# Two decoder blocks on one core: operands moved within 256 bytes, the even stage reordered, retention values in three passes

## The chip, the cores and the metric

One Trainium2 chip, one core of it. The metric is the device time of one execution in microseconds; lower is better. Float32 values are split into two parts of a shorter format (float32r), hi and lo, and most products are computed as hi·hi + hi·lo + lo·hi: three TensorE matmuls for each block of 128 rows.

## The reference, cut to what matters

A sequence of 256 tokens of width 1024 goes through a first block of 2 layers and a second of 2 layers; the second carries 256 context tokens beside the 256 latent ones (two streams).

```python
# first block, each of 2 layers
xn = rmsnorm(x, norm_mix[l])
qa..va, qb..vb, qc..vc, qi, ki, wi, gates = split(xn @ w_in[l])
y = g0 * (chunk_band(qa, ka, va) @ w_up_a) + g1 * (diff(qb, kb, vb) @ w_up_b) + g2 * (sparse(qc, kc, vc) @ w_up_c)
x = x + y @ w_out
x = x + memory_cross_attention(rmsnorm(x), mem)
x = x + (silu(h @ w_gate) * (h @ w_up)) @ w_down          # h = rmsnorm(x)

# second block, each of 2 layers; modulate(x) = rms_norm(x, gain) * (1 + scale) + shift
x = x + 0.5 * m2 * swiglu(modulate(x), ffn_a)              # both streams
# layer 0, "even": neighbourhood attention and a hyena operator
a = neighbourhood_attention(q, k, v, k_ctx, v_ctx, rpb)    # latent; the context attends to itself
z = x1 * x2                                                # short convolutions of three projections
b = (long_conv(z, filter) + z * hy_bias) * x0
x = x + m5 * (concat(a, b) @ even_out)
# layer 1: retention, latent stream alone in the output
inner = (q @ k.T) * decay;  o = inner @ v                  # both directions and the context's keys
x = x + m5 * ((silu(g) * groupnorm(o)) @ ret_out)
x = x + 0.5 * m8 * swiglu(modulate(x), ffn_b)
```

## The kernel before

**Layout.** Activations lie feature-major: 128 partitions of features, tokens along the free axis. A projection to feature-major output keeps the weights still and streams the activations (mm3, L296: lines 300, 301, 302, `fm_pair`, `fm2`, `fm2_split`, `down`), 256 columns where one stream runs and 512 where both do. A projection to token-major output (`tm_proj`, L405: lines 418 to 420) keeps the activations still and streams 512 columns of the weights; v of every attention, q, k and v of the even stage and v of retention go this way.

**Weights.** One list, `plan` (L1047), fixes the order of all 674 weight tiles of 128 x 1024. `Weights.pump` (L180) issues a tile's load on SP's queue (`raw`, 4 buffers), casts it to `whi` on ACT (L195) and subtracts to `wlo` on DVE (L196), 4 buffers each, as tiles before it are done with.

**Order.** The program is written as generators. `drive` (L265) takes a step of the main line (some 24 matmuls), then a step of a side line (attention, the index, hyena, norms) and of the modulation vectors (`mods`). TensorE runs the instructions in that order. Four PSUM banks (`acc`) hold projections, four (`aux`) all the rest.

**Places of the streamed operands.** They follow from the sizes of the tiles in the order of allocation. Bytes past a multiple of 256 at which the operand starts: `hh`, `hl` of the first block 192; `oh`, `yh`, `xoh` (attention outputs and mixed values) 64 in layer 0 and 96 in layer 1; `hidh`, `hidl` (gated hidden values) 64 in layer 0, 192 in layer 1 and 192 in the second block; `hh2`, `hl2` (named hh, hl in the profile, since they take that name) of the second block 224; `whi`, `wlo` 128, still or streamed. Consecutive 128-row blocks of an operand are 1024 or 2048 bytes apart, so the place is the same for all of them.

**The even stage** (`even`, L1603). z projections, transposed and handed to `hyena` (L1568) as a side line: a forward transform of 256 points by matmuls, a product with the filter's spectrum F on DVE (L1582 to L1587), an inverse transform (L1595), and z * hy_bias added (L1599). Beside it q, k, v; each of q and k is normed (L1658 to L1673) after its projection. Then neighbourhood attention of four pairs of heads and the context's own of four (`attention`, L536), its first steps beside the four x0 chunks, the rest by itself (L1710); then even_out.

**Retention** (`ret`, L1758). k, q, gates, then v, head by head; `ret_head` (L1857) computes the decays, the scores, the values as float32 matmuls (L1883, two records each), a norm over the head's width, and the gate. Then ret_out (L1846), `add_gated`, squares (`sq2`), and `norm2` (L1300): a sum over partitions on TensorE (L1305), a power on POOL (L341), a broadcast on TensorE (L1314), and `modulate` (L1326) with shift and scale. The last feed-forward stage (`ffn2`, L1394) calls `need_stream(0)` before its first matmul.

Of the kernel before, what the change touches and what calls it, by code (L numbers as in the profile page):

```python
# [17 lines left out]
P = 128  # L18
# [32 lines left out]
def layout(inp):  # L51
# [49 lines left out]
    o["w_mod"] = np.ascontiguousarray(f["w_mod_2"].transpose(0, 2, 1)).reshape(-1, P, D)  # L101
    o["cc"] = np.stack([f["c_2"][0], f["c_ctx_2"]])
# [4 lines left out]
def tables():  # L107
# [43 lines left out]
    o["rpos"] = np.ascontiguousarray(np.stack([np.maximum(i - j, 0), np.maximum(j - i, 0), 1.0 + (i == j), 256 + i - j, 256 - i + j], axis=1)).astype(np.float32)  # L151
# [4 lines left out]
EVEN_ORDER = [c for i in range(4) for c in (12 + 4 + i, 12 + 8 + i)] + list(range(12)) + [12, 13, 14, 15]  # L156
# [13 lines left out]

class Weights:
    S = 4
    R = 4

# [5 lines left out]
    def pump(self, limit=1 << 30):  # L180
        nc = self.nc
        moved = True
        while moved:
# [7 lines left out]
            if self.n_split < min(self.n_dma, self.n_done + self.S):  # L191
                raw = self.raw.pop(self.n_split)
                hi = self.pool.tile([P, 1024], F32R, tag="whi", name="whi", bufs=self.S)
                lo = self.pool.tile([P, 1024], F32R, tag="wlo", name="wlo", bufs=self.S)
# [18 lines left out]
class Prog:  # L213
# [214 lines left out]
    def scores(self, pr):  # L428
# [5 lines left out]
        e = self.att.tile([P, 2, w], F32, tag=pr.tag, name="e", bufs=2)  # L434
# [59 lines left out]
    def values(self, pr):  # L494
# [7 lines left out]
        if pr.rev:  # L502
            self.split(pr.oh.rearrange("p (t n) -> p t n", n=P), pr.ol.rearrange("p (t n) -> p t n", n=P), self.rev(ps[:, :T]))
        else:
            self.split(pr.oh, pr.ol, ps[:, :T])

# [462 lines left out]
    def ffn1(self, l):  # L969
        nc = self.nc  # L970
        x = (self.hh, self.hl)
        with ExitStack() as st:
# [8 lines left out]
            def gate(j, pa, pb):  # L981
                ga = tp.tile([P, 2, T], F32, tag="ga", name="ga")
                sg = tp.tile([P, 2, T], F32, tag="sg", name="sg")
                u = tp.tile([P, 2, T], F32, tag="u", name="u")
# [62 lines left out]
    def plan(self):  # L1047
# [52 lines left out]
        for i in range(16):  # L1100
# [4 lines left out]
    def setup(self):  # L1105
# [8 lines left out]
        nc.gpsimd.memset(self.mhalf, -0.5)  # L1114
        self.modT = [cp.tile([P, 9, 2, KC], F32, name=f"modT{l}") for l in range(2)]
    def setup1(self, st):
# [13 lines left out]
        self.bgain = cp.tile([P, 2], F32, name="bgain")  # L1130

# [104 lines left out]
    def setup2(self):  # L1236
# [5 lines left out]
        self.hl2 = cp.tile([P, KC, 2 * T], F32R, name="hl2")  # L1242

# [56 lines left out]
    def norm2(self, l, n, s, spread=False):  # L1300
# [12 lines left out]
        for t in range(2):  # L1313
            nc.tensor.matmul(ps[:, t * P:(t + 1) * P], rs[:, t:t + 1].to_broadcast([P, P]), self.ident, start=True, stop=True)  # L1314
        yield from self.modulate(l, n, s, lambda h, m: nc.vector.tensor_tensor(h, self.x2[:, m, s * T:(s + 1) * T], ps[:, :T], ALU.mult), spread)
# [9 lines left out]

    def modulate(self, l, n, s, normed, spread=False):  # L1326

        nc = self.nc
        shift, scale = self.need_mod(l, 3 * n), self.need_mod(l, 3 * n + 1)
        g = PAR["norm_gain"] + (l * 3 + n) * KC  # L1330
        gs = self.small2.tile([P, KC], F32, tag="gs", name="gs", bufs=2)
# [598 lines left out]
```

## Time and profile before

| | us |
|---|---|
| median of 3 runs | 2888.71 |
| lowest, highest | 2887.57, 2890.21 |
| the profiled execution | 2887.65 |
| its span, first to last instruction | 2885.7 |
| TensorE busy (18,228 matmuls) | 2855.2 |
| DVE, ACT busy | 2001.3, 1270.0 |

The granted TensorE clock is 0.997 of full speed over the span. Busy times of TensorE overlap, since matmuls are pipelined: an instruction lasts longer than the time until the next can start. How often one starts is read from a stretch in which a single loop runs: its length over the instructions in it.

### The profile page before, as it was taken

The numbers are of one execution on the slowest core, as the hardware profiler recorded it, in microseconds if no ns is written. First come the engines' busy times: TensorE is split into PE (matmuls) and PEld (weight loads), VectorE is DVE, ScalarE is ACT, GpSimd is POOL, SyncE is SP. The second block draws the span as 40 slices with busy tenths as digits, with TensorE's granted clock in tenths as the row PEclk, the third lists the DMA queues.
The fourth block names the chain that finished last, engine by engine and source line by source line (L and its number), as shares of the span: only waits on it lengthen the run. The fifth ranks groups of instructions, "written<-read, shape, count | busy, mean of one in ns | idle before, by whom it ended". The sixth has DMA issues, their size and how long they took to land.

```text
span 2885.7 us, 46572 instructions
## 1 busy us (share of the span) xinstructions
PE 2855.2 (99%) x18228; PEld 2523.8 (87%) x18228; DVE 2001.3 (69%) x3896; ACT 1270.0 (44%) x2002; POOL 77.9 (3%) x137
## 2 busy tenths in 40 slices
PE   8999999999999999999999999999999999999999
PEld 7899999989989988888876988888888888978999
DVE  7767898866878778784657566555887846535655
ACT  7666644677654532222436432123322235423543
POOL 0000000000000000000011000000000000000000
PEclk9999999999999999999999999999999999999999
DMA  7555577655656646553322244442565634522564
GB/s 229 161 163 168 196 237 244 188 146 159 197 174 211 220 152 187 187 185 98 111 73 66 81 146 141 144 153 88 158 188 185 188 92 136 161 68 91 159 187 147
DMA packets 150748, 452.04 MB, mean 157 GB/s; under 512 B 17183, under 2 KB 24936, under 8 KB 149760
## 3 DMA queue, kind: packets, MB, share of 16 engines
q1 hardware_dynamic: 147040, 435.94, 48.7%
q0 software_dynamic: 3344, 12.96, 1.4%
q8 instruction: 143, 2.34, 0.3%
q14 instruction: 77, 0.63, 0.1%
q10 hardware_dynamic: 144, 0.16, 0.0%
HBM read 447.94 MB, written 1.06 MB: 156 GB/s over the span
## 4 chain that ended last, share of the span: by engine, by line
PE 85%; issue 3%; DVE 2%; ACT 1%; POOL 0%; DMA 0%; POOLq 0%; DVEq 0%; ACTq 0%
PE acc L301 25%; PE acc L300 25%; PE acc L302 25%; PE acc L418 2%; PE acc L419 2%; PE acc L420 2%; PE aux L1883 1%; PE aux L489 1%; PE aux L501 1%; PE aux L1578 0%; PE aux L1876 0%; PE aux L442 0%; DVE wlo L196 0%; PE aux L1595 0%; DMA lg<-logit 0%
## 5 line engine op out<-in xcount | busy, mean ns | idle before, releaser
L195 ACT CAST whi<-raw 128x1024 fp32r<-128x1024 f32 x674 | 704.8, 1049 | 1344.4 <-PE acc L301 635.5
L300 PE MATMUL acc<-hh,whi 128*128 128x256 f32 (+1 forms) x3728 | 1167.7, 315 | 5.0 <-ACT hh L308 3.7
L196 DVE TENSOR_TENSOR wlo<-raw,whi 128x1024 fp32r<-128x1024 f32 x674 | 822.5, 1223 | 503.5 <-ACT whi L195 497.3
L301 PE MATMUL acc<-hl,whi 128*128 128x256 f32 (+1 forms) x3728 | 1166.5, 314 | 0.1
L302 PE MATMUL acc<-hh,wlo 128*128 128x256 f32 (+1 forms) x3728 | 1164.5, 314 | 0.0
L300 PEld LDWEIGHTS acc<-hh,whi 128*128 128x128 f32 x3728 | 699.1, 188 | 66.1 <-issue 7.7
L301 PEld LDWEIGHTS acc<-hl,whi 128*128 128x128 f32 x3728 | 701.7, 188 | 50.3 <-issue 0.8
L302 PEld LDWEIGHTS acc<-hh,wlo 128*128 128x128 f32 x3728 | 699.9, 188 | 46.6 <-issue 0.4
L1224 DVE CUSTOM_DVE_ANT_0 mjunk<-mraw,cb 128x512 f32<-128x512 f32 x576 | 396.4, 688 | 32.3 <-DMA mraw<-w_mod 20.9
L302 PE MATMUL acc<-hidh,wlo 128*128 128x256 f32 (+1 forms) x1152 | 370.4, 322 | 0.0
L301 PE MATMUL acc<-hidl,whi 128*128 128x256 f32 (+1 forms) x1152 | 370.3, 321 | 0.0
L300 PE MATMUL acc<-hidh,whi 128*128 128x256 f32 (+1 forms) x1152 | 368.8, 320 | 0.0
L301 PEld LDWEIGHTS acc<-hidl,whi 128*128 128x128 f32 x1152 | 216.3, 188 | 18.5
L300 PEld LDWEIGHTS acc<-hidh,whi 128*128 128x128 f32 x1152 | 216.3, 188 | 18.5
L302 PEld LDWEIGHTS acc<-hidh,wlo 128*128 128x128 f32 x1152 | 216.1, 188 | 16.6
L418 PE MATMUL acc<-whi,hh 128*128 128x512 f32 x320 | 131.7, 411 | 0.0
L420 PE MATMUL acc<-wlo,hh 128*128 128x512 f32 x320 | 127.0, 397 | 0.0
L419 PE MATMUL acc<-whi,hl 128*128 128x512 f32 x320 | 126.6, 396 | 0.0
L1412 DVE TENSOR_TENSOR u<-acc,u 128x512 f32<-128x512 f32 (+1 forms) x88 | 54.8, 624 | 79.6 <-PE acc L302 79.3
L1392 DVE SCALAR_TENSOR_TENSOR x<-acc,modT,x 128x256 f32<-128x256 f32 x136 | 59.6, 478 | 54.7 <-PE acc L302 54.7
L418 PEld LDWEIGHTS acc<-whi,hh 128*128 128x128 f32 x320 | 60.2, 188 | 17.0 <-issue 3.8
L419 PEld LDWEIGHTS acc<-whi,hl 128*128 128x128 f32 x320 | 60.3, 188 | 14.8 <-issue 1.4
(373 smaller groups left out, 2614.7 us busy)
## 6 DMA issues: line engine op xcount, KB each, us to landing
mraw<-w_mod SPq DMA_DIRECT2D x288, 256.0 KB, 3.1
raw<-w_in SPq DMA_DIRECT2D x126, 512.0 KB, 3.6
raw<-w_gu SPq DMA_DIRECT2D x88, 512.0 KB, 4.2
raw<-ffn_a_in SPq DMA_DIRECT2D x88, 512.0 KB, 3.5
raw<-ffn_b_in SPq DMA_DIRECT2D x88, 512.0 KB, 3.5
raw<-ret_in SPq DMA_DIRECT2D x48, 512.0 KB, 3.5
raw<-w_down SPq DMA_DIRECT2D x44, 512.0 KB, 4.1
raw<-ffn_a_out SPq DMA_DIRECT2D x44, 512.0 KB, 3.5
```

Source lines behind the costliest of these rows:

```text
L195: nc.scalar.copy(hi, raw)
L196: nc.vector.tensor_sub(lo, raw, hi.bitcast(F32))
L300: nc.tensor.matmul(out, wh, xh, start=first, stop=False)
L301: nc.tensor.matmul(out, wh, xl, start=False, stop=False)
L302: nc.tensor.matmul(out, wl, xh, start=False, stop=last)
L418: nc.tensor.matmul(o, xh[:, k, ts], wh[:, kk], start=first, stop=False)
L419: nc.tensor.matmul(o, xl[:, k, ts], wh[:, kk], start=False, stop=False)
L420: nc.tensor.matmul(o, xh[:, k, ts], wl[:, kk], start=False, stop=last)
L489: nc.tensor.transpose(pv[:, h, (t - t0) * P:(t - t0 + 1) * P], pr.e[t][:, h, kb * P:(kb + 1) * P], self.ident)
L1224: self.tc.keep_in_program_order(nc.vector.tensor_tensor_reduce(junk, w, cb[:, s, k * 512:(k + 1) * 512], 1.0, 0.0, ALU.mult, ALU.add, accu ...
L1392: nc.vector.scalar_tensor_tensor(xm, ps[:, ts], gate[:, s, m:m + 1], xm, ALU.mult, ALU.add)
L1412: nc.vector.tensor_tensor(u, pb, u, ALU.mult)
```

## The change

- **Places.** Pads (a tile that nothing uses) and a 64-column widening of the split weight tiles put every streamed float32r operand 64 bytes past a multiple of 256. Still operands of weights stay at 128 (`MOVING` adds 48 columns, 192 bytes, to weight tiles that are streamed). `hh` as a still operand goes to 64 with its streaming place.
- **Even stage.** Order q, k, v, then the z projections, then x0. The q projection takes the latent stream first, then the context's. Attention runs beside v and z and writes its output, unsplit, over q; hyena runs beside the x0 chunks, four steps behind each, in halves of 256 features. z * hy_bias goes into the real part of F. even_out begins with the attention's half of its rows.
- **Last feed-forward stage.** Its first two gated units (four weight chunks) are computed from x2 times the gain, not normed, as soon as ret_out is done, with shift as a 257th column (and a zero as a 258th); the row scale of the norm is applied to the PSUM result.
- **Retention.** The scores and v are split, and values are three float32r matmuls. A head's gate comes a step after its values. `ret_out` starts with chunks of heads 0 and 1. `rpos` has two tables in place of five. The first two heads of k are taken out of PSUM stream by stream.
- `ffn1`'s `u` has one buffer in place of two.

```diff
 class Weights:
+    ROOM, MOVING = 64, 48
+    def moves(self, key):
+        n, i = key[0], key[-1]
+        return (n == "w_kv" and i > 1 or n == "w_in" and key[2] in ("va", "vb", "vc")
+                or n == "even_in" and i < 12 or n == "ret_in" and 16 <= i < 32)
...
+                o = self.MOVING if self.moves(self.seq[self.n_split][0]) else 0
+                hi, lo = (self.pool.tile([P, 1024 + self.ROOM], F32R, tag=n, name=n, bufs=self.S)[:, o:o + 1024] for n in ("whi", "wlo"))
...
+def pad(pool, n):
+    pool.tile([P, n // 4], F32, name="pad")
...
+        pad(self.small, 128)       # setup
+        pad(cp, 128)               # setup1
+        pad(cp, 160)               # setup2
+        pad(fp, 224)               # filter_mlp
+        pad(np_, 224)              # even
+            pad(rp, 160)           # ret
...
 # ffn2, the last stage
+                    for j in range(2):
+                        pa, pb = self.head[2 * j:2 * j + 2]
...
+                        nc.vector.tensor_tensor(u, pa[:, :T], self.rsl, ALU.mult)
+                        nc.scalar.activation(sg, u, AF.Sigmoid, bias=sh[:, 0:1])
+                        nc.vector.scalar_tensor_tensor(u, u, sh[:, 0:1], sg, ALU.add, ALU.mult)
+                        t = tp.tile([P, ns], F32, tag="sg", name="ut2")
+                        nc.vector.tensor_tensor(t, pb[:, :T], self.rsl, ALU.mult)
+                        nc.vector.scalar_tensor_tensor(u, t, sh[:, 1:2], u, ALU.add, ALU.mult)
+                        self.split(hh[:, j], hl[:, j], u)
...
 # hyena, each half f of the features of each stream s
+                for kt in range(2):
...
+                    nc.vector.tensor_tensor(t1, pv, F[:, kt, f], ALU.mult)
+                    nc.vector.tensor_tensor(t2, pv, F[:, kt, f, ::-1], ALU.mult)
+                    nc.vector.tensor_tensor(Y[:, 0, kt], t1[:, 0], t1[:, 1], ALU.subtract)
+                    nc.vector.tensor_tensor(Y[:, 1, kt], t2[:, 0], t2[:, 1], ALU.add)
+                    yield
...
+                nc.scalar.copy(zT[:, 2 * s:2 * s + 2, fs], ps.rearrange("p (j t) -> p j t", j=2))
+                yield
...
 # even, the x0 chunks
             for i in range(4):
                 p, = yield from self.fm2([key(i)], x, 2 * T)
+                self.conv(p, i, u[:, i])
+                self.split(oh[:, i], ol[:, i], qT[:, i])
+                for _ in range(4):
+                    next(hy, None)
+                yield
...
 # ret
+            for m in range(2):
+                half(m, 0)
+                yield
+            next(heads)
+            ysplit(3)
...
+                with self.tc.high_priority(200):
+                    self.split_gain(xg[:, 0, m, :T], xg[:, 1, m, :T], self.x2[:, m, :T], gs[:, m:m + 1])
...
+            ws = [self.w.get(("ffn_b", 1, c), KC) for c in (0, NF, 1, NF + 1)]
+            self.head = [self.acc() for _ in ws]
+            for k in range(KC):
+                for (wh, wl), p in zip(ws, self.head):
+                    self.mm3(p[:, :T + 2], (wh[:, k], wl[:, k]), (xg[:, 0, k], xg[:, 1, k]), k == 0, k == KC - 1)
+                yield
...
 # ret_values
-                nc.tensor.matmul(ps, p[:, kt, t * P:(t + 1) * P], v[:, kt], start=kt == 0, stop=kt == 3)
+                nc.tensor.matmul(ps, ph[:, kt, ts], vh[:, kt], start=kt == 0, stop=False)
+                nc.tensor.matmul(ps, ph[:, kt, ts], vl[:, kt], start=False, stop=False)
+                nc.tensor.matmul(ps, pl[:, kt, ts], vh[:, kt], start=False, stop=kt == 3)
```

## Rows read from the trace of the kernel before

**Rows 1.** The page's first part: busy us (share of the span) x instructions of each engine.

```profile
PE 2855.2 (99%) x18228; PEld 2523.8 (87%) x18228; DVE 2001.3 (69%) x3896; ACT 1270.0 (44%) x2002; POOL 77.9 (3%) x137
```

**Rows 2.** The page's fourth part: the chain that ended last, shares by line.

```profile
PE acc L301 25%; PE acc L300 25%; PE acc L302 25%; PE acc L418 2%; PE acc L419 2%; PE acc L420 2%; PE aux L1883 1%; PE aux L489 1%; PE aux L501 1%; PE aux L1578 0%; PE aux L1876 0%; PE aux L442 0%; DVE wlo L196 0%; PE aux L1595 0%; DMA lg<-logit 0%
```

**Rows 3.** Groups by line and form: count | busy us, mean ns | idle before.

```profile
L300 PE MATMUL acc<-hh,whi 128*128 128x256 f32 x2672 | 752.2, 284 | 4.9 <-ACT hh L308 3.7 <-ACT xv L661 1.3
L302 PE MATMUL acc<-hh,wlo 128*128 128x512 f32 x1056 | 418.3, 396 | 0.0
L300 PE MATMUL acc<-hidh,whi 128*128 128x256 f32 x720 | 200.8, 279 | 0.0
L300 PE MATMUL acc<-hidh,whi 128*128 128x512 f32 x432 | 168.0, 389 | 0.0
L418 PE MATMUL acc<-whi,hh 128*128 128x512 f32 x320 | 131.7, 411 | 0.0
```

**Rows 4.** Stretches (us): length, then PE, PEld, DVE, ACT, POOL busy (count), PEclk, DMA.

```profile
455.00:510.00 55.00, 55.00 (x487) 55.00 (x487) 44.80 (x79) 24.39 (x27) 0.00 (x0) 1.00 0.76 239
945.00:1000.00 55.00, 55.00 (x470) 55.00 (x469) 39.80 (x67) 29.82 (x44) 1.21 (x2) 1.00 0.67 217
345.00:450.00 105.00, 105.00 (x894) 105.00 (x893) 98.04 (x167) 50.28 (x57) 0.00 (x0) 1.00 0.74 235
164.00:184.00 20.00, 20.00 (x179) 20.00 (x178) 10.78 (x12) 10.61 (x13) 0.00 (x0) 1.00 0.58 170
186.00:196.00 10.00, 10.00 (x87) 10.00 (x86) 6.96 (x8) 4.14 (x5) 0.00 (x0) 1.00 0.68 203
673.00:682.00 9.00, 9.00 (x78) 9.00 (x78) 5.91 (x7) 3.98 (x5) 0.00 (x0) 1.00 0.58 185
2700.00:2770.00 70.00, 70.00 (x585) 70.00 (x584) 44.90 (x64) 35.84 (x53) 0.00 (x0) 1.00 0.60 184
```

**Rows 5.** The same view of stretches with 512-column matmuls.

```profile
1035.00:1160.00 125.00, 125.00 (x537) 100.55 (x537) 108.08 (x237) 35.22 (x46) 0.00 (x0) 1.00 0.61 184
1170.00:1240.00 70.00, 70.00 (x308) 57.43 (x307) 51.24 (x122) 13.65 (x13) 0.00 (x0) 1.00 0.59 188
2504.00:2532.00 28.00, 28.00 (x121) 22.53 (x120) 6.73 (x7) 7.50 (x9) 0.00 (x0) 1.00 0.32 95
```

**Rows 6.** The same view of the retention values' stretch; the chain of waits there.

```profile
2498.00:2606.00 108.00, 108.00 (x463) 83.37 (x463) 38.76 (x49) 31.29 (x40) 3.19 (x8) 1.00 0.27 80
...
2617.56 6.88 PE aux L1883 x16
```

**Rows 7.** TensorE's timeline where retention ends: start us, us, what.

```profile
2684.35 0.28 PE L302 MATMUL acc<-hh,wlo 128*128 128x256 f32 x1
2687.29 0.61 PE L1305 MATMUL aux<-ones,ssq 128*128 128x1 f32 x4 [2.66 <-DVE ssq L1298]
...
2692.08 1.22 PE L300 MATMUL acc<-hh,whi 128*128 128x256 f32 x4 [1.93 <-ACT hh L308]
```

**Rows 8.** TensorE's waits at the end and at the start of retention.

```profile
PE aux L1897 <- DVE ry L1890: 1.4, 2, 0.7
...
PE acc L300 <- ACT hh L308: 1.7, 2, 1.4
```

**Rows 9.** Stretches again: the end of retention.

```profile
2684.00:2698.00 14.00, 8.38 (x52) 7.79 (x51) 8.01 (x21) 8.09 (x18) 0.70 (x1) 0.76 0.28 81
```

**Rows 10.** DVE's timeline in the hyena steps; groups by line and form.

```profile
1435.80 0.68 DVE L1582 TENSOR_TENSOR hyY<-aux,hyF 128x512 f32<-128x512 f32 x1
...
L309 DVE TENSOR_TENSOR hl<-modh,hh 128x256 fp32r<-128x256 f32 x88 | 34.4, 419 | 8.5 <-ACT hh L308 7.8
L1337 ACT ACTIVATE modh<-modh,modT,gs 128x256 f32<-128x256 f32 x88 | 49.3, 595 | 31.2 <-DVE modh L1315 23.0 <-DVE modh L1284 8.1
```

**Rows 11.** DMA issues at the start of retention: KB each, us to landing.

```profile
lg<-logit POOLq DMA_DIRECT2D x1, 4.0 KB, 9.5
```

**Rows 12.** Stretches again: the attention of the even stage.

```profile
1549.00:1593.00 44.00, 41.57 (x270) 27.50 (x270) 35.56 (x96) 33.45 (x87) 6.70 (x11) 1.00 0.18 54
```

More of the change, by code (lines that the diff above doesn't have):

```diff
@@ L1099, in plan @@
             add(("ret_in", i), a["ret_in"][i])
-        for i in range(16):
+        for i in [0, 2, 1, 3] + list(range(4, 16)):
             add(("ret_out", i), a["ret_out"][i])
@@ L1589, in hyena @@
-            for i in range(0, 4, 2):
+                    for part in range(2):
+                        for t in range(2):
+                            nc.tensor.matmul(ps[:, part * T:(part + 1) * T], self.dft[:, part, t, kt * P:(kt + 1) * P], zT[:, 2 * s + t, fs], start=t == 0, stop=t == 1)
+                    pv = ps.rearrange("p (a c) -> p a c", a=2)
+                    t1, t2 = (self.cp.tile([P, 2, T], F32, tag="conv", name=n, bufs=2) for n in ("ctm", "ctp"))
+                    nc.vector.tensor_tensor(t1, pv, F[:, kt, f], ALU.mult)
@@ L1660, in even, with flip @@
                     gain = self.pcol("na_k_gain", 0) if part else qgain
-                    for t in range(4):
+                    def flip(t, raw, rs, gain, part):
                         r = raw[:, t].rearrange("p (h d) -> p h d", h=8)
@@ L1668, in even @@
                         ts = slice(t * P, (t + 1) * P)
-                        if part == 0:
-                            dst = qT[:, :, ts]
-                            nc.scalar.activation(dst[:, :, ::-1] if t < 2 else dst, pv, AF.Copy, scale=gain)
-                        else:
-                            nc.scalar.activation(k[:, :, ts], pv, AF.Copy, scale=gain)
-                        yield
-                def evac(t, p):
-                    nc.scalar.copy(v[:, t], p)
-                yield from self.tm_proj([("even_in", 8 + i) for i in range(4)], x, 4, evac)
-                while "hyena" not in self.flags:
-                    self.step_side()
-            self.Fst.close()
-            self.att = pool("naatt", st)
+                        dst = k[:, :, ts] if part else qT[:, :, ts]
+                        nc.scalar.activation(dst[:, :, ::-1] if part == 0 and t < 2 else dst, pv, AF.Copy, scale=gain)
+                    for t in range(4):
+                        self.defer(lambda t=t, c=(raw, rs, gain, part): flip(t, *c), 1)
+                yield
+                self.flush_later()
             pairs = []
@@ L1719, in f @@
                         then(s, m0 + i)
-                return f
-            for m0 in (0, 4):
-                yield from self.fm2_split([("even_out", m0 + i) for i in range(4)], x, (0, 1), after(m0))
     def na_bias(self, pr):
@@ new lines, in ret, with evac @@
+            heads = self.ret_heads(rp, rpos, lg, qT, kT, vs, sg)
+            self.side.append(heads)
+            for h in range(4):
+                vs.append(())
+                def evac(t, p):
+                    if t == 0:
+                        vs[h] = tuple(rp.tile([P, 4, 512], F32R, tag=n, name=n, bufs=1) for n in ("rvh", "rvl"))
+                    self.split(vs[h][0][:, t], vs[h][1][:, t], p)
+                yield from self.tm_proj([("ret_in", 16 + 4 * h + i) for i in range(4)], x, 4, evac)
@@ new lines, in ret, with half @@
+            gs = self.mod_gain(1, 2, 0)
+            nc.vector.memset(xg[:, :, :, T + 1:].bitcast(F32), 0.0)
+            self.split(xg[:, 0, :, T], xg[:, 1, :, T], self.need_mod(1, 6)[:, 0])
+            psums = {}
+            def half(m, kg):
+                if kg == 0:
+                    psums[m] = self.acc()[:, :T]
+                wh, wl = self.w.get(("ret_out", 2 * m + kg), KC)
+                for k in range(KC):
+                    self.mm3(psums[m], (wh[:, k], wl[:, k]), (yh[:, 8 * kg + k], yl[:, 8 * kg + k]), kg == k == 0, kg == 1 and k == KC - 1)
+                self.w.done()
@@ L1858, in ret_head, with ret_decays @@
+    def ret_decays(self, h, rp, rpos, lg):
         nc = self.nc
@@ L1907 @@
     pt_bufs = 2
+    e_bufs = 2
+    out = None
     rev = False
```

348 lines of the change are left out of this document (219 added, 129 removed).

## Prediction

> **What bounds the kernel now.** I read the page's busy lines first, then the chain of waits, then TensorE's groups by line, then the stretches of single loops, and last the timeline of the few gaps. TensorE has work under way for 99% of the span [rows 1], and three quarters of the chain that ends last are the three matmuls of one helper, L300 to L302 [rows 2]: the time is nearly the sum of the start-to-start times of 18,228 TensorE instructions. So what decides is how often a matmul can start. I take this from a stretch in which one loop runs: its length over the number of instructions in it, less 2 for those that cross its edges (an instruction lasts some 281 ns and starts every 118, so two are in flight at an edge).
>
> For 256 columns the same down projection takes 55 us / 485 = 113.4 ns in layer 0, where its streamed operand starts 64 bytes past a multiple of 256, and 55 / 468 = 117.5 ns in layer 1, where it starts at 192 [rows 4]. The weights, the loop and the clock (1.00) are alike. The gate loop of layer 0, from 192, takes 105 / 892 = 117.7; layer 1's oh, from 96, 9 / 76 = 118.4; block 2's hh, from 224, 70 / 583 = 120.1. Two rows speak against a plain rule of the address: hh from 192 runs at 20 / 177 = 113.0 in one stretch, and ohc, from 64, at 10 / 85 = 117.6 [rows 4]. There seem to be a fast and a slow steady pattern; from 64 the fast one is the more frequent, from 192 the rare one, and from 96 and 224 there is a third, slower one. For 512 columns [rows 5] the pairs are 125 / 535 = 233.6 from 224, 70 / 306 = 228.8 from 192 and 28 / 119 = 235.3 for streamed weights from 128.
>
> **The change part by part: streamed operands at 64.** Counts are the rows of L300 to L302 times three [rows 3]. Of the 2672 with hh and 256 columns, 1120 lie in block 2 (from 224: gate and up chunks of the split and the last feed-forward stage 544, retention 384, even projections 192), so 1552 lie in block 1 (from 192). Of hidh's 720, 176 in layer 0 start at 64 already. From 192 there are then 1552 + 176 + 368 = 2096 triples, 6288 matmuls; from 224 3360; from 96 176 triples (oh, yh, xoh of layer 1), 528. With 512 columns: 3168 of hh, 1296 of hidh, 960 streamed weights.
> What share from 64 will be fast? In the rows one stretch of two, and 485 of 570 matmuls; I take 0.7, so 0.7 x 113.4 + 0.3 x 117.5 = 114.6 ns. From 192 the rows have 177 of 1537 fast, a mean of 117.1.
> - From 192: 2.5 x 6288 = 15.7 us; none if slow, 23.3 if all are fast.
> - From 224: 5.5 x 3360 = 18.5 us; 8.7 if slow (117.5), 22.5 if fast.
> - From 96: 3.8 x 528 = 2.0 us; 0.5 and 2.6.
> - 512 columns from 64 no row shows. The floor would be twice the fast 256, 226.8; the nearest row is 228.8. I take 228: 5.6 x 3168 = 17.7, 0.8 x 1296 = 1.0, 7.3 x 960 = 7.0, together 25.7 us. The ends are 33 (all at 226.8) and, if the place does nothing for 512, 0. For streamed weights the stationary operand (hh) moves to 64 too, a pair that stands in no row, so a loss isn't excluded there; by the spread of the 512 rows, 6.5 ns, it would be 6 us.
> Sum 61.9 us, between 3 (slow pair, 512 unchanged, the loss of 6) and 81. No work hides this: TensorE is the chain.
> The trace's rows tell the five starts apart. The Trainium skill ("SBUF — State Buffer", Specifications (TRN2)) names a 16-byte line as the unit that costs when it is crossed. All of the starts are multiples of 32 bytes, so by that rule they are alike, this sum is nothing, and what is left is the third rival below; layer 0 against layer 1 [rows 4] speaks against it.
>
> **Retention values in three passes.** Now 64 records of L1883, 16 in 6.88 us [rows 6], 27.5 us. After: 4 heads x 2 x 4 x 3 = 96 matmuls of 512 columns at 228, 21.9 us: 5.6 us less. Added beside it are 24 casts on ACT and 24 subtractions on DVE of 512 (16 for v, where a plain copy was, 8 for p), at 0.69 [rows 10] 16.6 us of DVE, in a stretch of 108 us in which DVE is busy 38.8 and ACT 31.3 [rows 6]: hidden. If it weren't, at most the 16.6 would come back. The start of the heads' steps moves by one step each; the transposes of y now come one step behind the values, so that the two waits for ry, 1.4 us [rows 8], go; for the last head two half chunks of ret_out (48 matmuls, 5.5 us) stand between.
>
> **Last gated unit un-normed.** Now the last matmul of ret_out starts at 2684.35, the first of the last feed-forward stage at 2692.08 [rows 7]: 7.6 us, of which 8 small matmuls take 0.9. The granted clock of that stretch is 0.76 [rows 9]; the next 13 matmuls run at half clock, 13 x 0.1 = 1.3 us more. Together 8.0 us lost. After: four chunks' matmuls (96, of 258 columns) read the scaled, un-normed x and need no norm. In order on TensorE behind the first 12 of them comes the sum of squares, which was ready 2.94 us after the last matmul [rows 7], so it still waits 2.94 - 12 x 0.12 = 1.5 us. The broadcast comes some 36 matmuls in; behind it ACT and DVE have 8 modulated chunks (each an activation of 0.6 and a cast on ACT, two of 0.42 on DVE [rows 10]), some 8 us, then the first gate unit. But the head holds all four acc banks until its gate units read them, and only 60 matmuls (7 us) are left to cover: the next chunk waits some 3 us. So 4.5 of the 8.0 stay: 3.5 us less. If the banks come late by the whole 8 us, 0; if nothing waits, 8.
>
> **Smaller pieces.** Start of retention: TensorE waits 1.7 us for hh [rows 8] behind ACT, which stands at the exponential of lg; lg lands 9.5 us after its issue [rows 11], in one queue behind axC and axS of 256 KB and rpos of 5 x 512 x 4 x 128 bytes, 1280 KB. rpos becomes 512 KB; at that queue's pace (1792 KB in some 9.5 us) lg comes some 4 us earlier and most of the wait goes: 1.5 us less (0 to 1.7). The two products of 8 columns that are added there stand behind the same DMA, off TensorE's path.
> Even stage: the same matmuls of the hyena steps, in other widths. Attention moves beside the value and z projections, where DVE has room. That closes part of the 2.4 us in which TensorE has nothing in 1549 to 1593 [rows 12], and some waits inside it that the busy time covers: 3 us less (0 to 6). In exchange hyena's twelve steps, now one between matmuls of a projection, are issued four at a time after each x0 chunk. An inverse step right behind its forward step waits for two products of 512 and two sums of 256 on DVE: 2 x 0.69 + 2 x 0.42 = 2.2 us [rows 10]. Three such waits bare: 6.6 us, with partial cover 4 more (0 to 9). The direct term's 256 KB and its two sums come in the filter's stage of block 1, beside the cross attention, where F is not yet wanted; the pads are space alone.
>
> **Sum.** 61.9 + 5.6 + 1.4 + 3.5 + 1.5 + 3 - 4 = 72.9 us, against the profiled execution's 2887.65 (span 2885.7 and 1.95 around it): 2814.8. The median of the runs shown, 2888.71, is 1.1 above it: 2816.
>
> **Rivals.**
> 1. The slow pattern stays: from 64 the matmuls settle at 117.5 as ohc does [rows 4], and only the starts at 224 and 96 gain. 8.7 + 0.5 for 256; 512 at the row of 192, 228.8: 4.8 x 3168 + 6.5 x 960 = 21.4. With the 11 us of the other parts 41.6 less: 2847. For it: a loop that begins slow stays slow for its 96 matmuls. Against: layer 0's down projection came out of a slow gate loop and ran fast.
> 2. All settle fast: 81 + 11 less, 2797. For it: 485 matmuls on end. Against: ohc.
> 3. The place of the operand is worth nothing, and the two rates come from something else that differs between the layers: 11 less, 2878.
> 4. Slower: hyena's steps lie bare. All eight forward steps' 2.2 us of DVE and four copies of 0.6 on ACT stand between matmuls: 20 us on the path of the even stage, and the 3 us there are not won. The parts outside that stage give 12.0 (5.6 + 1.4 + 3.5 + 1.5), so it makes the kernel slower from where the operands give less than 8 us; with rival 3 it is 2888.7 - 12 + 20 = 2897. For it: nothing stands between the four steps but what another chunk of x0 lends. Against: each chunk gives 5.5 us of cover, and DVE was busy for 0.81 of the stretch with the most attention in it [rows 12].
>
> **How the numbers follow.** Forecast 0.62 (2816, own range 2797 to 2838), rival 1 0.17, rival 2 and below 0.07, rival 3 0.08, rival 4 0.06. The range for 8 in 10 leaves out the far end of rival 2 and rivals 3 and 4: 2788 to 2866. A measurement of this kernel tells 0.2%, 6 us, from no change. Rival 3 at 11 us is faster by that bound, with a few hundredths of it within: faster 0.91, same 0.03, slower 0.06.
>
> **What would show it.** The stretches of the gate loops: windows of hh with 256 columns at 113 to 115 ns a matmul (right), or at 117.5 throughout (rival 1) or 120 in block 2 (rival 3). 512 columns at 227 to 229 in the feed-forward stages of block 2. L1883's successor at 228 a matmul, with no wait for the split of v. Between ret_out and the last stage two gaps of 1.5 and 3 us in place of 7.6, and a clock of 1.00. In the x0 chunks of the even stage waits of TensorE for hyY: up to four of 2 us is the forecast, eight or more is rival 4. The prediction is wrong where the 512-column matmuls don't move at all, since a third of the sum rests on them without a row.

## The result, and the profile after

The changed kernel takes 2857.46 us (median of 4 runs, 2852.39 to 2860.48), the kernel before in the same job 2889.46: a ratio of 0.9888, with a 95% interval of 0.9871 to 0.9905, 32 us less. The forecast was 73 us less. The time lies inside the range and outside the likeliest case's own one.

The profiled execution takes 2852.39 us. First its page: busy time by engine, answering to [rows 1], and the chain that ended last by line, answering to [rows 2].

```profile
PE 2820.6 (99%) x18196; PEld 2502.3 (88%) x18196; DVE 2018.8 (71%) x3935; ACT 1284.2 (45%) x2030; POOL 76.0 (3%) x131
...
PE acc L313 25%; PE acc L314 25%; PE acc L315 25%; PE acc L431 2%; PE acc L433 2%; PE acc L432 2%; PE aux L514 1%; DVE wlo L209 1%; PE aux L502 1%; ACT whi L208 1%; PE aux L1644 0%; PE aux L2049 0%; PE aux L1631 0%; PE aux L455 0%; ACT modh
```

L313 to L315 are now the three matmuls of the helper, L431 to L433 those with streamed weights. TensorE is still under way for 99%, so the time went, or stayed, in the interval between two starts. The stretches of single loops, columns as in [rows 4]: first 256 columns (layer 0's gates and down projection, layer 1's, block 2's last gates, and the retention gates), then 512 columns as in [rows 5] (hh, hidh, streamed weights), and last the end of retention, as in [rows 9].

```profile
345.00:450.00 105.00, 105.00 (x894) 105.00 (x893) 97.25 (x166) 50.47 (x57) 0.00 (x0) 1.00 0.77 236
455.00:510.00 55.00, 55.00 (x470) 55.00 (x469) 42.79 (x77) 24.38 (x27) 0.00 (x0) 1.00 0.74 230
825.00:930.00 105.00, 105.00 (x928) 105.00 (x927) 88.61 (x129) 51.97 (x58) 0.00 (x0) 1.00 0.71 219
945.00:995.00 50.00, 50.00 (x430) 50.00 (x429) 35.56 (x61) 27.74 (x42) 1.26 (x2) 1.00 0.66 208
2685.00:2740.00 55.00, 55.00 (x487) 55.00 (x487) 37.47 (x55) 27.64 (x42) 0.00 (x0) 1.00 0.64 196
2428.00:2485.00 57.00, 57.00 (x505) 57.00 (x504) 40.93 (x48) 32.59 (x39) 0.00 (x0) 1.00 0.64 194
1030.00:1150.00 120.00, 120.00 (x516) 96.67 (x515) 104.93 (x230) 33.74 (x44) 0.00 (x0) 1.00 0.60 184
1165.00:1230.00 65.00, 65.00 (x281) 52.35 (x280) 48.05 (x113) 11.61 (x11) 0.00 (x0) 1.00 0.58 183
2491.00:2518.00 27.00, 27.00 (x121) 22.48 (x121) 12.32 (x16) 10.71 (x14) 0.00 (x0) 1.00 0.30 93
2673.00:2683.00 10.00, 8.03 (x53) 7.60 (x52) 8.97 (x18) 8.96 (x14) 0.00 (x0) 0.83 0.47 166
```

Every stretch has its streamed operand at 64 now. Three of the loops run at 113 ns (layer 1's gates 105 / 926 = 113.4, block 2's last gates 55 / 485 = 113.4, the retention gates 57 / 503 = 113.3) and two at 117.5 (layer 0's gates 105 / 892 = 117.7, its down projection 55 / 468 = 117.5). Layer 1's down projection, 50 / 428 = 116.8, has both: 117.8 up to 961 us, where four small matmuls break in, then 113.5 up to the next such break at 970 us, then 117.8 again. So 64 does not choose. Layer 0's down projection, fast before [rows 4], is slow now, though its operands have not moved. And 512 columns: 120 / 514 = 233.5, where 233.6 stood [rows 5]; hidh 65 / 279 = 233.0, which was 228.8; only the streamed weights gained, 27 / 119 = 226.9 against 235.3.

All means below are of intervals between successive starts in the trace, without those over 150 ns (256 columns) or 260 (512), in which something was waited for; where the matmuls run by themselves, of the settled later part of a stretch.

Next the waits of TensorE, in three stretches: the end of retention, its start, and the even stage (what is waited for: us in total, times, longest), with the DMA issue of lg, as in [rows 8] and [rows 11].

```profile
PE acc L313 <- DVE u L1454: 1.5, 1, 1.5
PE acc L313 <- ACT whi L208: 0.4, 1, 0.4
...
PE acc L313 <- ACT modh L1365: 2.1, 1, 2.1
PE aux L1335 <- POOL nrs L354: 0.5, 1, 0.5
PE aux L1326 <- DVE ssq L1319: 0.4, 1, 0.4
...
PE aux L455 <- DVE m L472: 1.1, 1, 1.1
PE aux L1335 <- POOL nrs L354: 0.5, 1, 0.5
PE aux L1719 <- DVE naraw L1716: 0.4, 1, 0.4
...
lg<-logit POOLq DMA_DIRECT2D x1, 4.0 KB, 4.1
```

At the end of retention the waits of 2.7, 1.0 and 1.9 us for sums, broadcast and first modulated chunk are gone, and one of 1.5 for the gate unit's product (u) has come. At its start lg lands after 4.1 us, not 9.5, and the wait for hh behind it is gone; the first matmul now waits 2.1 us for the modulated chunk itself (modh), and the sums (ssq) are waited for 0.4 us. In the even stage no wait is for hyY.

### The profile page after: what moved, and what is told of

It is laid out like the page before. It is cut to its first block, busy times and chain, and to the rows that moved or that the text cites. A ratio compares the mean times of both kernels' runs of the same rounds, so it can differ in the third digit from the quotient of the medians.

```text
span 2850.2 us, 46574 instructions
## 1 busy us (share of the span) xinstructions
PE 2820.6 (99%) x18196; PEld 2502.3 (88%) x18196; DVE 2018.8 (71%) x3935; ACT 1284.2 (45%) x2030; POOL 76.0 (3%) x131
## 4 chain that ended last, share of the span: by engine, by line
PE 86%; DVE 2%; ACT 2%; issue 1%; POOL 1%; DMA 0%; ACTq 0%; DVEq 0%; POOLq 0%
PE acc L313 25%; PE acc L314 25%; PE acc L315 25%; PE acc L431 2%; PE acc L433 2%; PE acc L432 2%; PE aux L514 1%; DVE wlo L209 1%; PE aux L502 1%; ACT whi L208 1%; PE aux L1644 0%; PE aux L2049 0%; PE aux L1631 0%; PE aux L455 0%; ACT modh L1365 0%
## 5 line engine op out<-in xcount | busy, mean ns | idle before, releaser
L313 PE MATMUL acc<-hh,whi 128*128 128x256 f32 (+1 forms) x3600 | 1135.1, 316 | 5.6 <-ACT modh L1365 2.1
L314 PE MATMUL acc<-hl,whi 128*128 128x256 f32 (+1 forms) x3600 | 1129.8, 314 | 0.0
L315 PE MATMUL acc<-hh,wlo 128*128 128x256 f32 (+1 forms) x3600 | 1129.0, 314 | 0.0
L313 PEld LDWEIGHTS acc<-hh,whi 128*128 128x128 f32 x3600 | 677.6, 189 | 67.3 <-issue 9.3
L315 PEld LDWEIGHTS acc<-hh,wlo 128*128 128x128 f32 x3600 | 678.4, 189 | 51.7 <-issue 2.7
L314 PEld LDWEIGHTS acc<-hl,whi 128*128 128x128 f32 x3600 | 678.5, 189 | 50.1 <-issue 0.4
L313 PE MATMUL acc<-hidh,whi 128*128 128x256 f32 (+1 forms) x1152 | 371.9, 323 | 0.0
L315 PE MATMUL acc<-hidh,wlo 128*128 128x256 f32 (+1 forms) x1152 | 371.6, 323 | 0.0
L315 PEld LDWEIGHTS acc<-hidh,wlo 128*128 128x128 f32 x1152 | 217.2, 189 | 19.6
L313 PEld LDWEIGHTS acc<-hidh,whi 128*128 128x128 f32 x1152 | 216.7, 188 | 19.8 <-DVE u L1007 0.2
L431 PE MATMUL acc<-whi,hh 128*128 128x512 f32 x288 | 116.1, 403 | 0.0
L433 PE MATMUL acc<-wlo,hh 128*128 128x512 f32 x288 | 113.2, 393 | 0.0
L322 DVE TENSOR_TENSOR hidl<-u,hidh 128x512 fp32r<-128x512 f32 (+1 forms) x110 | 69.4, 632 | 0.8 <-ACT hidh L321 0.7
L321 ACT CAST hidh<-u 128x512 fp32r<-128x512 f32 (+1 forms) x110 | 63.2, 576 | 9.9 <-DVE u L1440 4.9
```

What stands on the lines that cost most here:

```text
L313: nc.tensor.matmul(out, wh, xh, start=first, stop=False)
L314: nc.tensor.matmul(out, wh, xl, start=False, stop=False)
L315: nc.tensor.matmul(out, wl, xh, start=False, stop=last)
L321: self.nc.scalar.copy(hi, src)
L322: self.nc.vector.tensor_sub(lo, src, hi.bitcast(F32))
L431: nc.tensor.matmul(o, xh[:, k, ts], wh[:, kk], start=first, stop=False)
```

## The experiments

The question is where 41 us of the forecast stayed. Theory A, from the comparison: 512-column matmuls gain nothing from the streamed operand's place alone. Theory B: the places gave what was forecast, and another edit took it back.

**Places alone, the rest alone, and the changed kernel again.** The first is the kernel before with:

```diff
+    ROOM, MOVING = 64, 48
-                hi = self.pool.tile([P, 1024], F32R, tag="whi", name="whi", bufs=self.S)
+                o = self.MOVING if self.moves(self.seq[self.n_split][0]) else 0
+                hi, lo = (self.pool.tile([P, 1024 + self.ROOM], F32R, ...)[:, o:o + 1024] for n in ("whi", "wlo"))
-                u = tp.tile([P, 2, T], F32, tag="u", name="u")
+                u = tp.tile([P, 2, T], F32, tag="u", name="u", bufs=1)
+        pad(self.small, 128)
+        pad(cp, 128)
+        pad(cp, 160)
+        pad(fp, 224)
```

Its one buffer for `u` stays in the second kernel too, and no run shows what that alone is worth.

> The kernel before with the streamed operands moved to 64 and nothing else. Theory A (512 columns gain nothing, the 256-column matmuls gain about 31 us, the other edits about 5): 26 to 34 us under the kernel before, near 2858. Theory B (the places gave what was forecast, some 55 to 62 us, and the other edits cost 20 to 27): near 2830. In its trace theory A has the 512-column matmuls of the feed-forward and retention stages at a mean of 233 to 234 ns, theory B at 226 to 227.

The second is the changed kernel with `ROOM, MOVING = 0, 0` and without its six pads.

> The changed kernel with its padding taken out and every operand back at its old place: the other edits alone. Theory A: 3 to 10 us under the kernel before, near 2883. Theory B: 15 to 27 us over it, near 2910.

The third is the changed kernel as it is.

> The changed kernel once more, unaltered. Theory A2 (whether a stretch of 256-column matmuls settles at 113 or at 118 ns is decided anew at each entry by small offsets in time): the profiled execution has some of its stretches in the other pattern than the first one (the first layer's gates from 338 us, slow, and its first feed-forward part from 452 us, slow), and the times spread by 0.2 to 0.4%. Rival B2 (the program fixes it): the same stretches are slow, to within a few dozen matmuls, and the times agree within 0.1%.

Places alone: 2869.71 us (2858.85 to 2875.56), ratio 0.9931 (0.9905 to 0.9956), 19 us less. The rest alone: 2873.13, ratio 0.9946 (0.9929 to 0.9963), 16 us less. Together 35; so nothing was taken back and theory B falls. Theory A's numbers were off too (31 and 5 expected), but its mark holds: with the places alone, 512 columns keep means of 233.3 (hh) and 233.3 (hidh, from 228.9), and streamed weights go from 233.9 to 227.9.

The changed kernel again: 2854.41 (2849.45 to 2859.30). Its long loops settle as before, the gates of layer 0 slow and those of layer 1 fast. The first three rows are layer 0's gates and down projection and layer 1's gates, the last the retention gates:

```profile
345.00:450.00 105.00, 105.00 (x894) 105.00 (x893) 98.06 (x167) 49.95 (x57) 0.00 (x0) 1.00 0.73 235
455.00:510.00 55.00, 55.00 (x470) 55.00 (x469) 43.03 (x76) 23.70 (x27) 0.00 (x0) 1.00 0.71 234
825.00:930.00 105.00, 105.00 (x928) 105.00 (x927) 88.33 (x129) 52.40 (x59) 0.00 (x0) 1.00 0.69 218
2428.00:2485.00 57.00, 57.00 (x486) 57.00 (x486) 41.27 (x50) 31.38 (x37) 0.00 (x0) 1.00 0.59 185
```

The retention gates went the other way, 57 / 484 = 117.8 against 113.3. Matmul by matmul, 26% of the 256-column intervals are in the other pattern than in the first execution. So neither theory is right alone: program and execution both have a part in the choice. Within a run of matmuls that nothing interrupts the choice holds: the two executions have 117 such runs of 24 to 1492 matmuls, and the means of 113 of them lie either at 113.3 to 114.0 ns or at 117.7 to 117.9.

**The matmuls by themselves, over places.** The model is left out:

```diff
+for n, mv, st in [(n, mv, st) for n in (256, 512) for mv in range(8) for st in range(8)]:
+    for k in k8:
+        m, ml = (x[:, 8 * mv + k * n:8 * mv + k * n + n] for x in (xh, xl))
+        s, sl = (w[:, 8 * st + k * 128:8 * st + k * 128 + 128] for w in (wh, wl))
+        for a, b in ((s, m), (s, ml), (sl, m)):
+            nc.tensor.matmul(ps[:, :n], a, b, ...)
```

> Leaves the model out and runs only float32r matmuls in the kernel's three-pass pattern, 48 of 256 columns and 36 of 512 columns twice for each of 64 pairs of places (streamed and still operand, 32 bytes apart within 256). Theory A (the 512-column time depends on both operands' places): streamed 64 with still 128 gives a mean of 233 to 234 ns from start to start, streamed 64 with still 64 gives 226.7, streamed 224 with still 128 about 233. Theory B (the streamed place alone decides, and the 226.7 of the streamed weights has another cause): at streamed 64 all eight still places give one value within 1 ns. For 256 columns both expect 113.3 or 117.7 at streamed 64 with still 128, and near 120 at streamed 64 with still 64.

512 columns in four stretches of 15 us: streamed 192 with still 128, 224 with 128, 64 with 128, and 64 with 64.

```profile
1007.00:1022.00 15.00, 15.00 (x67) 12.33 (x66) 0.16 (x1) 0.00 (x0) 0.00 (x0) 1.00 0.00 0
1141.00:1156.00 15.00, 15.00 (x66) 12.06 (x65) 0.16 (x1) 0.00 (x0) 0.00 (x0) 1.00 0.00 1
1542.00:1557.00 15.00, 15.00 (x66) 12.02 (x65) 0.16 (x1) 0.00 (x0) 0.00 (x0) 1.00 0.00 0
1642.00:1657.00 15.00, 15.00 (x68) 12.43 (x67) 0.16 (x1) 0.00 (x0) 0.00 (x0) 1.00 0.00 1
```

One or two matmuls more in 15 us are the effect. Sorted by the difference of the two places (streamed less still, within 256 bytes), the 64 means of 512 columns fall into nearly one value each: 226.7 at 0, 228.8 at 64, 232.3 to 232.8 at 128 (one pair 233.5), 234.2 at 160, 233.2 to 233.5 elsewhere. The kernel's 233.4 (224 against 128), 228.9 (192 against 128), 233.3 (64 against 128) and 227 (64 against 64) are four points of it. Theory A holds; the streamed place alone decides nothing.

**512 columns put right.** Only the set of weights that are shifted grows:

```diff
-                or n == "even_in" and i < 12 or n == "ret_in" and 16 <= i < 32)
+                or n == "even_in" and i < 24 or n == "ret_in" and 12 <= i < 32
+                or n in ("ffn_a", "ffn_b") and key[1] + (n == "ffn_b") < 2 and i not in (0, 1, NF, NF + 1)
+                or n in ("ffn_ao", "ffn_bo") and key[1] + (n == "ffn_bo") < 2 and (key[2] == 0 or i < FGROUPS[1][0] // 2))
```

> The changed kernel with the still weights of the 512-column stages also put at 64, so that streamed and still operand stand at the same place within 256 bytes there; the 256-column stages keep their still weights at 128. Theory A (the difference decides): the activations' 512-column matmuls go from 233.3 to 226.7 ns, 3242 x 6.6 = 21.4 us, the feed-forward values' 1296 x 6.6 = 8.6 us, so 30 us less than the changed kernel, near 2826, less by up to 6 where faster matmuls wait more. Rival E (in the kernel other traffic sets the 233): within 5 us of the changed kernel, near 2855, with means of 232 to 234.

2825.94 us (2823.77 to 2828.48), ratio 0.9785 (0.9769 to 0.9801): near 2826, as expected, and 28 to 32 us under the two medians of the changed kernel (30 expected). That it is met to 0.1 us is luck, since executions of one kernel differ by several us. The stretches of hh and hidh with 512 columns, 110 / 485 = 226.8 and 65 / 286 = 227.3:

```profile
1035.00:1145.00 110.00, 110.00 (x487) 91.09 (x486) 98.73 (x219) 31.39 (x40) 0.00 (x0) 1.00 0.62 192
1150.00:1215.00 65.00, 65.00 (x288) 53.83 (x287) 50.09 (x121) 13.10 (x13) 0.00 (x0) 1.00 0.58 190
```

**256 columns: the entry, and finer places.** Here the first measurement had left 116.7 to 120 for 63 of the 64 pairs, 117.8 for most of those at a difference of 64 or 192. A short matmul of changing width stands ahead of each stretch:

```diff
+for n, mv, kick in ROWS:                    # mv in 16-byte steps, still at 128
+    nc.tensor.matmul(kk[:, :64 + 8 * kick], wh[:, 0:128], xh[:, 0:64 + 8 * kick], start=True, stop=True)
+    ...                                     # 48 matmuls as above
```

> Leaves the model out: the still operand stays at 128, the streamed one moves in 16-byte steps, and ahead of each stretch of 48 matmuls of 256 columns stands one short matmul of 64, 72, up to 152 columns (12 entries per place); 36 matmuls of 512 columns once per place. Theory C (the difference of the two places decides the set of patterns, and at differences of 64 and of 192 bytes a stretch settles by its entry at 113 or at 118 ns and stays there): at 192 (streamed at 64) some of the 12 entries give 113.3 and the rest 117.7, hardly one a value between; at 0 all give 120. Rival D (the entry doesn't matter, something else in the program chose): all 12 entries of a place agree within 0.5 ns. For 512 columns both expect 226.7 at a difference of 0, 229 at 64, 232 to 234 elsewhere.

Means of the 12 entries by difference (at 0 of nine):

```
difference   mean of each entry, ns
0            120.0 at all
64           117.8 at all
112          113.3 at all
192          113.3 117.8 117.8 113.3 113.3 117.8 113.3 117.8 113.3 117.8 117.8 117.8
```

At 192, which is the changed kernel's pair, 5 entries of 12 settle at 113.3 and 7 at 117.8: theory C. But 112 looked as if it could not fail, so it went into two kernels. In both, the still weights of 256-column stages move to 208 and those of 512 to 64:

```diff
-                o = self.MOVING if self.moves(self.seq[self.n_split][0]) else 0
+                o = self.place(self.seq[self.n_split][0])     # 48 for 512 columns, 20 for 256
```

> The changed kernel with every still operand put by the difference: at the streamed one's place for 512 columns (as in the run before), and 112 bytes behind it (streamed 64, still 208) for 256 columns, where all 12 entries of the measurement settled at 113.3 ns. Theory C (the difference decides in the kernel too): 256 columns at 113.3 to 113.8 in every stage, which takes 8659 x 2.0 + 2147 x 2.3 + 90 x 6.5 ns = 23 us out of the matmuls; as in the run with the places alone a quarter comes back as waits, so 17 us under the 2825.9 of the run with 512 columns put right: 2809, and a spread of the times under 0.15%. Rival F (waits and other traffic in the kernel break the pattern again and again): a mean of 115 or more, 2821 or more.

> The kernel before with places alone, both differences put right as in the other kernel of this call (0 for 512 columns, 112 for 256), nothing else of the change. Theory C: 8909 x 5.0 + 2149 x 3.3 ns of 256 columns, 3157 x 6.6 + 1296 x 2.3 + 916 x 6.0 ns of 512, together 81 us, less a quarter of the first two in waits, so 68 us: near 2821. If the places as such were worth little (the 19 us of the first run with places alone was all there is): near 2865.

A plain miss: 2861.09 us (0.9903, 0.9887 to 0.9920) where 2809 was expected, and 2875.10 (0.9954, 0.9939 to 0.9969) where 2821 was. 512 columns are at 226.8 in both; 256 columns rose to means of 119.3 and 119.7. Layer 0's and layer 1's gates in the first of them, 105 / 875 = 120.0:

```profile
345.00:450.00 105.00, 105.00 (x877) 105.00 (x876) 95.92 (x164) 50.33 (x57) 0.00 (x0) 1.00 0.70 229
825.00:930.00 105.00, 105.00 (x878) 104.87 (x877) 84.93 (x122) 53.41 (x66) 1.63 (x1) 1.00 0.62 198
```

Within the first the 96 matmuls with streamed weights at 176 and still memh at 64, the same difference, had 115 and the rest 119: a hint that the place itself counts as well.

The places by themselves, finer:

```diff
-STEP = 4          # 16 bytes
+STEP = 2          # 8 bytes
```

> Leaves the model out: the measurement of places in 8-byte steps, 5 entries each for 256 columns. Theory C: 113.3 ns for all entries at 112 and in some window round it, either 113.3 or 117.8 at 192; 512 columns 226.7 at 0 and above 228 from 16 bytes on. If 112 were a lucky point rather than a window, 104 and 120 read 116 or more.

In 8-byte steps 112 is a point, not a window: 113.3 there, 120.0 at 104 and 120.1 at 120. At 192 three entries of five are fast. 512 columns: 226.7 at 0, 232.6 at 8.

And a grid that moves both operands:

```diff
-                x0, w0 = mv * STEP + k * n, k * 128
+                x0, w0 = mv * STEP + k * n, st * STEP + k * 128    # STEP = 4, 16 x 16 places
```

> Leaves the model out: the measurement of places once more, now with both operands moved in 16-byte steps over all 16 x 16 pairs, three entries each for 256 columns and one for 512. In the two model kernels with still operands at 208 the 256-column matmuls alternated at 119.5 ns, where the measurement at the same difference (streamed 240, still 128) had 113.3. Theory G (the absolute place counts too: the streamed operand must stand at an odd multiple of 16 bytes for the pattern of 112 to hold): at a difference of 112, all pairs with the streamed operand at 16, 48, 80 and so on give 113.3 and all with it at 0, 32, 64 give 119 to 120. Rival H (the difference alone counts and the kernel's surroundings broke the pattern): all 16 pairs of that difference give 113.3. For 512 columns both have 226.7 on the whole diagonal.

256 columns, three entries a pair, rounded means; "even" and "odd" are the streamed operand's place in units of 16 bytes:

```
difference   streamed even                   streamed odd
112          120 in 23 of 24, one 118        113 in all 24
192          113 in 15 of 24, else 118       113 in all 24
```

512 columns: with the streamed operand even, 226.7 at differences of 0 and 16 (15 of 16 pairs); odd, 226.6 at 64 and at 224 (16 of 16), and 230 to 233 at 0. Theory G is right and rival H (the difference alone) wrong. For 512 columns both had expected the whole diagonal at 226.7; half of it is. Both 256-column pairs in one view, 64 against 208 and 80 against 224 (13.0 and 12.4 us, of three entries with their short matmuls):

```profile
2590.60:2603.60 13.00, 13.00 (x110) 13.00 (x110) 0.47 (x3) 0.00 (x0) 0.00 (x0) 1.00 0.01 1
2813.30:2825.70 12.40, 12.40 (x111) 12.40 (x111) 0.47 (x3) 0.00 (x0) 0.00 (x0) 1.00 0.01 1
```

**The grid's rule in the kernel.** Streamed activations at 80; still weights at 16 for 512 columns (difference 64) and, for 256, at 224 (difference 112) or at 144 (192). Where the weights are streamed they stand at 144, their still operand at 80 (64 again):

```diff
+def odd(pool, k, n, **kw):
+    return pool.tile([P, k * n + 64], F32R, **kw)[:, 4:4 + k * n].rearrange("p (k n) -> p k n", k=k)
-        self.hh = hp.tile([P, KC, T], F32R, name="hh")
+        self.hh = odd(hp, KC, T, name="hh")
...
+        return 36 if wide else 24       # the other kernel: 4
```

> The changed kernel with all streamed operands at 80 (an odd multiple of 16 bytes), the still weights at 224 for 256 columns (difference 112) and at 16 for 512 columns (difference 64); two temporary tiles are saved to make the room, with as many operations as before. Theory G (the grid holds in the kernel): 256 columns at 113.3 to 114 in every stage, 512 at 226.7; against the kernel with 512 columns put right (2825.9) 8659 x 2.0 + 2147 x 2.3 + 90 x 6.5 ns = 23 us less, a quarter of it given back as waits: near 2809. Rival F (the kernel's waits and traffic break the pattern): 115 to 119 for 256 columns, 2826 or more.

> The same with the still weights of 256 columns at 144 (difference 192, streamed at an odd multiple of 16 bytes: all 48 entries of the grid settled at 113.3, against 37 of 48 with the streamed operand at an even one). Theory G: the same as its neighbour, near 2809, with 256 columns at 113.3 to 114 and no stage in the 118 pattern. Rival (the choice between 113 and 118 at a difference of 192 is chance whatever the streamed place): 115.1 as in the changed kernel, near 2826.

(By the grid's table it is 24 of 24 against 15 of 24, not 48 and 37 of 48.) 2809.42 us (2808.78 to 2809.95, ratio 0.9719, 0.9706 to 0.9733) and 2807.72 (2806.99 to 2808.82, ratio 0.9715, 0.9702 to 0.9728): 48 and 50 us under the changed kernel. 256 columns have means of 113.9 and 113.6, 512 columns 226.7. The stretches of the second: layer 0's gates and down projection, layer 1's gates, and 512 columns of hh.

```profile
345.00:450.00 105.00, 105.00 (x929) 105.00 (x928) 101.36 (x174) 52.25 (x59) 0.00 (x0) 1.00 0.78 247
455.00:510.00 55.00, 55.00 (x485) 54.79 (x484) 44.24 (x80) 26.55 (x32) 1.56 (x4) 1.00 0.77 239
825.00:930.00 105.00, 105.00 (x927) 104.82 (x926) 91.61 (x136) 51.88 (x59) 0.00 (x0) 1.00 0.71 220
1025.00:1140.00 115.00, 115.00 (x509) 95.27 (x508) 102.69 (x228) 33.63 (x44) 0.00 (x0) 1.00 0.63 194
```

The spread shrank as well: 2849 to 2859 for the changed kernel again, under 2 us for each of these. In the second no uninterrupted run of 24 or more is left in the 118 pattern. One group kept 120 ns, the un-normed head's matmuls of 258 columns (119.8 in the changed kernel, 120.1 and 120.3 here): their 128-row blocks are 258 columns, 1032 bytes, apart, so each starts 8 bytes further than the one before within 256. The change did not bring them to 64, and the table in 8-byte steps would account for the 120, but no run moves them.

**The un-normed head alone.** The changed kernel without it:

```diff
-            ws = [self.w.get(("ffn_b", 1, c), KC) for c in (0, NF, 1, NF + 1)]
-            self.head = [self.acc() for _ in ws]
...
-                    self.split_gain(xg[:, 0, m, :T], xg[:, 1, m, :T], self.x2[:, m, :T], gs[:, m:m + 1])
```

> The changed kernel with the last gated unit's first two pairs on normed values again, as before the change. By the stage times (the stretch from the end of the retention output to the end of the last gates was 5.2 us shorter with the other edits alone) 5 us over the changed kernel, near 2861; by the prediction's term 3.5 us over, near 2859; if the un-normed head only moves its wait, the same 2856.

2854.90 us (2852.21 to 2855.57): by the time alone the third answer, the same. But that kernel's 256 columns settled fast more often (a mean of 114.8 against 115.1 of hh and its like, 115.1 against 115.5 of hidh, 8735 and 2147 matmuls: 3.3 us), which is as large as the effect. From the last matmul of ret_out to the end of the next stage's first group of gates it takes 85.7 us, the changed kernel 82.2 and 80.6 in its two executions. So the total is inconclusive; by the stage the head gives 3.5 to 5.1. The stall it removes, back in this kernel (columns as in [rows 7]):

```profile
2660.59 0.28 PE L315 MATMUL acc<-hh,wlo 128*128 128x256 f32 x1
2663.53 0.60 PE L1326 MATMUL aux<-ones,ssq 128*128 128x1 f32 x4 [2.66 <-DVE ssq L1319]
2665.16 0.71 PE L1335 MATMUL aux<-ident,nrs 128*128 128x128 f32 x4 [1.03 <-POOL nrs L354]
2667.81 0.58 PE L313 MATMUL acc<-hh,whi 128*128 128x256 f32 x1 [1.93 <-ACT hh L321]
```

## Why the prediction was wrong, step by step

The bound was right: the time is the sum of the starts' intervals. The step that failed is "512 columns from 64 no row shows ... I take 228". It took the floor from the fast 256-column rate and the streamed operand's place for the cause; from 64 against 128 the kernel with places alone measured 233.3, and this term of 25.7 us came to nothing. In every row with streamed activations the still weights stood at 128, so no row could tell the streamed operand's own place from its distance to the still one, and the still operand's place was left out as alike. 512-column matmuls that don't move are also the sign of being wrong that the prediction gave itself; those with streamed activations did not gain. The terms of the places, with what the kernel with places alone measured against the kernel before, matmul by matmul:

```
term                          forecast   measured, us less
256 columns from 192          15.7       10.3
256 columns from 224          18.5       17.9
256 columns from 96            2.0        2.3
256 columns at 64 already      0         -2.0
512 columns, hh               17.7        0.1
512 columns, hidh              1.0       -5.7
512 columns, streamed weights  7.0        5.5
intervals with a wait in them  0         -6.1
sum                           61.9       22.3
```

The fp32 matmuls and transposes took 1.5 more, so 20.8 are accounted for; the profiled execution is 20.5 shorter (2887.65 to 2867.11), the medians differ by 19.4.

- 512 columns, 25.7 forecast, 0 came (-0.1 in the sum of its three terms). The end of the range that was given for this (0, and a loss for the streamed weights) had the sign of the loss at the wrong term: hidh lost, since 192 against 128 (difference 64) is a better pair than 64 against 128.
- 256 columns: the two patterns, 113.4 and 117.5, were read rightly, the share of 0.7 from too few stretches. After the move 43% of those from 192 and 75% of those from 224 were fast. Whether a stretch settles fast is set at its entry; layer 0's down projection, fast before, lost 2.
- Not priced: 6 us came back as longer waits. That faster matmuls wait longer for producers that are no faster is the likely reason, argued and not shown. It is no fixed share: where the 512-column matmuls were put right, their intervals gave 29.8 us and the waits grew by nothing; with the grid's rule on top 17 to 19 us came off the 256-column intervals and 3 came back.
- That 61.9 us lie in the places was nearly right by luck, at other places: the kernel with the grid's rule stands 65 us under the rest alone (2873.13 to 2807.72), with 46 from 256 columns, where 36 were forecast, and 30 from 512, less what came back. Rival 1 (2847) had the size better than the forecast did, and the wrong reason: it has 512 columns gain 21.4 and 256 only 9.2.

The Trainium skill ("TensorE: Matmul & The Clock Gate", Step-by-step: what each phase is for) has the streamed and the still operand read through two independent ports. By that alone their relative place would not matter. The trace differs: the 6.6 ns of 512 columns between differences of 0 and 192 speak against it, and no run here shows the mechanism.

The other parts were forecast at 11.0 us. The rest alone measured 12.1 in its profiled execution (2887.65 to 2875.59) and 16 by the medians. By the places in both traces where one stage hands over to the next:

- Retention values and the end of retention: 7.0 forecast, 7.4 measured. The values take 96 x 226.8 ns = 21.8 us, and no wait for the split of v is seen beyond 0.3.
- Un-normed head: 3.5 forecast, 5.2 with the rest alone. 4.5 of the 8.0 us were to stay; in the changed kernel waits of 1.5 and 0.4 stay, 17 matmuls behind them at some 0.21 us each, 1.7 us more than at 0.113 (granted clock 0.83, against 0.76 in [rows 9]), and 0.6 for the 96 matmuls at 120 ns: about 4. The wait for the sum of squares, put at 1.5, did not come: 25 matmuls of the head stand ahead of it (from 2661.2 to 2664.4 us, more than the 2.94 us that the sum needs), where the prediction had 12.
- Start of retention: 1.5 gain forecast, 1.6 loss measured. The DMA did come earlier, and the wait was replaced by one for the modulated chunk, 1.7 with the rest alone; and one for the sum of squares came, 1.4 (0.4 and 1.6 in the changed kernel's two executions). The next late thing was not asked for.
- Even stage: 1 loss forecast, 2.2 gain measured. None of the four waits for hyY came.

## What to carry to other kernels

Where TensorE's interval is the time, look at the places of both operands of a matmul, and at pairs, before moving one; a table of the two places taken from the matmuls alone costs one run and says what a kernel's rows can't. When two rates stand side by side in one loop with the same shapes, take it for a choice made at entry, and look for a place at which all entries agree, rather than for a mean. Price also what faster matmuls will wait for: here, of 28 us from faster 256-column starts, 6 came back, and of 30 from 512-column ones none.

## What the hardware showed that was not expected

- For float32r matmuls with 128 still columns the interval depends on where both operands start: 226.7 to 236.9 ns with 512 columns and 113.3 to 120 with 256 (means of a pair, over 16-byte steps), at a granted clock of 1.00 over that run.
- At a difference of 192 bytes with the streamed operand at an even multiple of 16 there are two steady patterns of 256 columns, 113.3 and 117.8; a stretch enters one and stays until something interrupts it. At an odd multiple all 24 measured entries took the first.
- A difference 8 bytes beside a good one loses all or most of it: 112 gives 113.3 for 256 columns, 104 and 120 give 120; 0 gives 226.7 for 512, 8 gives 232.6.
